# A decoder layer in fp32 on one core: the banded branch of half 0 by seven products in place of eight, with its sums of outputs made beside the last gate tiles

## The chip, the cores and the metric

The kernel runs on one core of a Trainium2 chip. The metric is the device time of one execution in microseconds (us); "before" is the median of three runs. The core has five engines that run at the same time, each its own instruction stream: TensorE (PE, with PEld for its weight loads), VectorE (DVE), ScalarE (ACT), GpSimd (POOL) and SyncE (SP). SP issues nearly all transfers between device memory and SBUF, on one queue, in order. TensorE writes only to PSUM, which has eight banks here; VectorE and ScalarE empty them.

## The reference, cut to what matters

A hybrid decoder layer: 2048 tokens with 16 meta tokens ahead of them, width 1024. One input projection yields queries, keys and values of two attentions, and gates. The stick-breaking attention has 8 heads of 64, the banded one ("sliding window", 128 wide) 16. What comes after them is what the change touches:

```python
y_sb = (o_sb * jax.nn.silu(sb_z)) @ w_branch_sb[l]     # 512 -> 1024
y_sw = (o_sw * jax.nn.silu(sw_z)) @ w_branch_swa[l]    # 1024 -> 1024, the "banded branch"
merged = jax.nn.sigmoid(g_sb) * y_sb + jax.nn.sigmoid(g_sw) * y_sw
h = h + merged @ w_out[l]
return rms_norm(h, final_norm_gain)[:, BLOCK:]
```

## The kernel before, in words

Every tile has 128 partitions. The tokens are taken in four groups of 512 columns, in reverse order, in two halves: half 0 is groups 2 and 3, half 1 is groups 0 and 1. Each fp32 operand x is split into a high part h (a rounded copy, fp32r) and a low part l = x - h, and each product is three matmuls that add up in one bank: h.h, h.l and l.h. A tile of 128 output columns with 1024 inputs is thus 8 x 3 = 24 matmuls of 512 columns per group.

`tile_kernel` computes projections and attentions of half 0, then of half 1, and last `finish` (line 235) for both halves. The gates (silu of sb_z and sw_z, sigmoid of g_sb and g_sw) are tiles of the input projection; `gate` (line 612) takes such a product from a bank with the tag "g" (two banks), applies ScalarE's sigmoid (line 615) and, for silu, a product on VectorE (line 617), and stores it to device memory (`zs`, `zw`, `gs`, `gw`). Attention outputs lie there too (`ow` banded, `od` stick-breaking).

The last five gate tiles of half 1 (the last of g_sw and four of sb_z) come after all attention, in the loop at line 1457. After each of the first four, the kernel makes ready four of the 16 tiles of gated banded outputs of half 0: `gated` (line 206) loads output and gate, multiplies (217), copies the high part (ScalarE, 219) and subtracts for the low part (VectorE, 220); they stay in SBUF as `ringl`. Line 1469 splits the first weight tile of w_sw (`weights`, line 178, with `split`, line 112). Then the buffers of x and of temporary tiles are given back (`fst.close()`), and `finish` takes that place for its own.

In `finish`, for each half: (1) the banded branch, for each of eight tiles d of 128 columns and each of the two groups 24 matmuls (`project`, lines 258 to 260, reading `ringl`), then a product with the gate `gw` (286) into `part`; the weights are split on GpSimd (lines 117 and 123) and in half 0 also stored in split form, which half 1 loads again; (2) between, the outputs of the other branch (`od`) made ready in the same way, into `ringr` (277); (3) the other branch, 12 matmuls per tile and group, reading `ringr`, product with `gs`, sum with `part`, split into `merged` (296 to 300); (4) the product with w_out (336 to 338), residual, norm, store. Weights of w_out are split by `out_weights` (265), the second half of them after the first output tile (349). While half 0's outputs are made, half 1's banded outputs are made ready in place (`gated_in_place`).

The order on TensorE is that of the program text. The order on VectorE, ScalarE, GpSimd and SP is chosen by a scheduler that models their times, except where the code says `manual_schedule`; each engine then works its list off in order, and an instruction waits for semaphores of the others.

Of the kernel before, what the change touches and what calls it, by code (L numbers as in the profile page):

```python
# [43 lines left out]
def f32(ap):  # L44
    return ap.bitcast(F32)
# [3 lines left out]
def tile_kernel(ctx, tc, x, xt, meta, metat, gain, w_in, w_sb, w_sw, w_out, sinks, fgain,  # L49
# [6 lines left out]
    V, A, G, T = nc.vector, nc.scalar, nc.gpsimd, nc.tensor  # L56

    def DMA(dst, src):
        nc.sync.dma_start(*(t.bitcast(F32) if t.dtype == F32R else t for t in (dst, src)))
# [34 lines left out]
    def dram(name, shape, dt=F32):  # L94
        return dp.tile(shape, dt, tag=name, name=name)
# [79 lines left out]
        DMA(raw, w[c0 // P])  # L175
        return raw

    def weights(c0, w=w_in, raw=None, split=split):
# [11 lines left out]
        split(wh, wl, raw)  # L190
        kept[key] = [dram(f"{t}_{w.name}_{c0}", [P, n, P], F32R) for t in "hl"]
# [9 lines left out]

    def rings():
        lp = cst.enter_context(tc.tile_pool(name="cl", bufs=1, side="left"))
        return lambda dt=F32R: lp.tile([P, GT], dt, tag="L", name="ringl", bufs=32)

    def gated(src, zz, k, g, ring, stg):

# [24 lines left out]
        V.tensor_tensor(l, t, f32(h), op=ALU.subtract)  # L232
        return h, l

    def finish(ringl, osw, first):
        cp = cst.enter_context(tc.tile_pool(name="wb", bufs=1, side="right"))
        banks = iter(range(1 << 30))

        def bank():
            return ps("gzt"[next(banks) % 3])  # L240

        def ringr(dt=F32R):
            return cp.tile([P, GT], dt, tag="R", name="ringr", bufs=40)

        def small(tag, bufs):
            return cp.tile([P, GT], F32, tag=tag, name=tag, bufs=bufs)
# [15 lines left out]
        for half, groups in enumerate(halves):  # L262
            part, merged, wo = {}, {}, {}

            def out_weights(k, ch):
                raw = small("a", AB)
                DMA(raw, w_out[0, k * P:(k + 1) * P, ch * GT:(ch + 1) * GT])
                h, l = wo[k, ch] = ringr(), ringr()
                A.copy(h, raw)
                V.tensor_tensor(l, raw, f32(h), op=ALU.subtract)  # L270

            osw2 = {}
            ws_of = {}
            order = [(d, g) for ds in ([0, 1, 2], *([d] for d in range(3, 8))) for g in groups for d in ds]
            for d, g in order:
                if d == 3 and g == groups[0]:
                    osb = {(k, g): gated(od, zs, k, g, ringr, lambda: small("a", AB)) for g in groups for k in range(4)}
                if d not in ws_of:
                    ws_of[d] = first if half == d == 0 else weights(d * P, w_sw)
# [4 lines left out]
                DMA(gt, gw[d][g])  # L284
# [4 lines left out]
            for d in range(8):  # L289
                ws = weights(d * P, w_sb)  # L290
                for g in groups:
                    acc = bank()
                    project(acc, ws, [osb[k, g] for k in range(4)])
                    gt = small("gt", 3)
                    DMA(gt, gs[d][g])
                    V.tensor_tensor(gt, acc, gt, op=ALU.mult)
                    V.tensor_tensor(gt, gt, part[d, g], op=ALU.add)  # L297
                    mh, ml = merged[d, g] = ringl(), ringl()
                    A.copy(mh, gt)  # L299
                    V.tensor_tensor(ml, gt, f32(mh), op=ALU.subtract)  # L300
                if d < 6:
                    out_weights(d + 2, 0)
            for g in groups:
                for t0 in range(0, 4, 2):
                    res, ssq, scaled_by = {}, {}, {}
# [12 lines left out]
                    for ch in range(2):  # L318
                        cs = slice(ch * GT, (ch + 1) * GT)
                        for t in (t0, t0 + 1):  # L320
                            row = g * GT + t * P
                            if ch == 0:
                                res[t] = cp.tile([P, D], F32, tag="xr", name="res", bufs=3)
                                DMA(res[t], x[row:row + P, :])
                            ts = slice(t * P, (t + 1) * P)
                            last = end and t == 3
                            if ch == 0:
                                ssq[t] = cp.tile([P, 2], F32, tag="ssq", name="ssq2", bufs=4)
                            sum_of = ssq[t][:, ch:ch + 1]
# [19 lines left out]
                            if (g, t, ch) == (groups[0], 0, 0):  # L349
                                for k in range(KT):  # L350
                                    out_weights(k, 1)
# [44 lines left out]
    def sums():  # L396
        return tp.tile([P, 2, 4], F32, tag="ssq", name="ssq", bufs=3)
# [953 lines left out]
    for half, groups in enumerate(halves):  # L1351
# [100 lines left out]
            mid.close()  # L1452
        else:
            ringl = rings()
            osw = {}
            todo = [(k, g) for g in halves[0] for k in range(8)]
# [10 lines left out]
            for k, g in todo:  # L1467
                osw[k, g] = gated(ow, zw, k, g, ringl, tmp)
    first = weights(0, w_sw)
    fst.close()  # L1470
    finish(ringl, osw, first)
    cst.close()

_OUT = (2048, 1024)
# [45 lines left out]
```

## Time and profile before

| | us |
|---|---|
| median of 3 runs (2090.64 to 2091.54) | 2091.31 |
| the profiled execution's own time | 2093.26 |
| its span, first to last instruction | 2091.4 |
| TensorE busy in the span | 2076.3 |
| VectorE busy | 1463.0 |
| ScalarE busy | 1091.4 |
| GpSimd busy | 345.7 |

The profile comes from one execution, whose time is 1.95 us above the median of the others. A matmul's record is longer than the step to the next one, because matmuls overlap; so a busy TensorE says that there was no gap, and the step from start to start gives the price. In rows of a stretch the engines are PE, PEld, DVE, ACT and POOL, each with its busy time and number of instructions; behind them stand the granted TensorE clock (1.00 is full), the busy share of the 16 DMA engines, and GB/s. In rows of single instructions stand start, duration, engine, line, operation, what it writes and reads, its shapes, and in brackets how long the engine was idle before and whom it waited for.

### The profile page before, as it was taken

The page shows a single profiled execution, that of the slowest core. Times are in us where ns is not written, and L with a number is a line of the kernel's source. Part 1 is how long each engine was busy: PE and PEld are TensorE (multiplying, and loading weights), DVE is VectorE, ACT ScalarE, POOL GpSimd, SP SyncE. Part 2 cuts the span into 40 slices and gives each one's busy share as a digit, 9 for nine tenths or more (in the row PEclk, how much of TensorE's full clock was granted, in tenths as well). Part 3 has the DMA queues.
Part 4 walks back from the last instruction along what each step waited for, and adds up shares of the span by engine and source line. Part 5 has one row for each costly group of instructions (what it writes and reads, how often), then busy time and mean ns, then how long its engine had stood idle before and what let it go on. Part 6 is the DMA issues. An engine that isn't in the chain of part 4 may idle for free. (4 is left out here: it accounts for less than half of the span.)

```text
span 2091.4 us, 30949 instructions
## 1 busy us (share of the span) xinstructions
PE 2076.3 (99%) x10579; PEld 1744.8 (83%) x10579; DVE 1463.0 (70%) x2383; ACT 1091.4 (52%) x2657; POOL 345.7 (17%) x682
## 2 busy tenths in 40 slices
PE   9999999999999999999999999999999999999998
PEld 7888888888888888888888888888888888788887
DVE  7897986877687754887728788777774547464543
ACT  6677774577665335777735555655653212321121
POOL 1233444331000000233310000000000343000000
PEclk9999999999999999999999999999999999999999
DMA  9855555866377574435455344343424987568532
GB/s 338 307 195 201 188 175 179 252 199 185 91 278 298 209 247 163 159 126 177 150 171 161 120 130 129 114 129 98 121 83 165 350 318 223 182 229 305 154 100 91
DMA packets 170093, 391.46 MB, mean 187 GB/s; under 512 B 23728, under 2 KB 28208, under 8 KB 169936
## 3 DMA queue, kind: packets, MB, share of 16 engines
q1 hardware_dynamic: 169648, 389.23, 55.8%
q8 instruction: 83, 1.36, 0.3%
q14 instruction: 74, 0.61, 0.1%
q10 hardware_dynamic: 288, 0.27, 0.0%
HBM read 241.68 MB, written 145.18 MB: 185 GB/s over the span
## 5 line engine op out<-in xcount | busy, mean ns | idle before, releaser
L464 PE MATMUL ps_g<-xh,wh 128*128 128x512 f32 x1264 | 517.0, 409 | 1.1 <-DVE tmp L680 0.6
L464 PE MATMUL ps_g<-xl,wh 128*128 128x512 f32 x1264 | 495.6, 392 | 0.7 <-DVE xl L1199 0.6
L464 PE MATMUL ps_g<-xh,wl 128*128 128x512 f32 x1264 | 495.7, 392 | 0.0
L928 DVE TENSOR_TENSOR_SCAN row<-row 128x512 f32<-128x512 f32 (+4 forms) x256 | 290.1, 1134 | 116.2 <-POOL row L923 60.1
L464 PEld LDWEIGHTS ps_g<-xh,wl 128*128 128x128 f32 x1264 | 237.8, 188 | 52.7
L464 PEld LDWEIGHTS ps_g<-xh,wh 128*128 128x128 f32 x1264 | 238.5, 189 | 39.9 <-ACT xh L1198 1.4
L464 PEld LDWEIGHTS ps_g<-xl,wh 128*128 128x128 f32 x1264 | 239.2, 189 | 38.0 <-DVE xl L1199 1.8
L921 ACT ACTIVATE row<-ps_z 128x512 f32<-128x512 f32 (+4 forms) x352 | 175.1, 509 | 159.3 <-PE ps_z L918 155.0
L126 ACT ACTIVATE wth<-ps_t 128x512 fp32r<-128x512 f32 (+1 forms) x320 | 171.6, 536 | 61.4 <-PE ps_t L943 59.6
L127 DVE SCALAR_TENSOR_TENSOR wtl<-ps_t,wth 128x512 fp32r<-128x512 f32 (+1 forms) x320 | 188.7, 590 | 21.3 <-ACT wth L126 20.7
L918 PE MATMUL ps_z<-kt,q 128*128 128x512 f32 (+4 forms) x704 | 183.7, 349 | 2.0 <-ACT row L921 1.9
L943 PE MATMUL ps_t<-ident,row 128*128 128x128 f32 x1088 | 171.4, 273 | 1.0 <-DVE wtl L127 0.9
L943 PEld LDWEIGHTS ps_t<-ident,row 128*128 128x128 f32 x1088 | 134.5, 140 | 33.1 <-DVE wtl L127 1.8
L918 PEld LDWEIGHTS ps_z<-kt,q 128*128 128x128 f32 x704 | 124.4, 188 | 27.4 <-ACT row L921 5.1
L975 PE MATMUL ps_o<-wth,vc 128*128 128x512 f32 (+1 forms) x320 | 131.2, 410 | 0.0
L975 PE MATMUL ps_o<-wtl,vc 128*128 128x512 f32 (+1 forms) x320 | 116.4, 364 | 0.0
L767 ACT ACTIVATE sc<-sc,nm 128x129 f32<-128x129 f32 x256 | 100.0, 393 | 30.5 <-DVE nm L765 29.5
L934 POOL COPY mr<-row 128x16 f32<-128x16 f32 x128 | 28.4, 224 | 444.2 <-DVE row L928 401.8
L615 ACT ACTIVATE tmp<-ps_g 128x512 f32<-128x512 f32 x80 | 48.0, 600 | 80.5 <-PE ps_g L464 74.3
L299 ACT CAST ringl<-gt 128x512 fp32r<-128x512 f32 x32 | 19.9, 621 | 127.1 <-DVE gt L297 93.3
L117 POOL TENSOR_SCALAR wh<-raw 128x1024 fp32r<-128x1024 f32 (+1 forms) x45 | 49.8, 1108 | 212.7 <-PE ps_g L464 90.3
L123 POOL TENSOR_TENSOR wl<-raw,wh 128x256 fp32r<-128x256 f32 x88 | 83.2, 975 | 2.0
(442 smaller groups left out, 4202.3 us busy)
## 6 DMA issues: line engine op xcount, KB each, us to landing
wh<-h_in_w_in SPq DMA_DIRECT2D x66, 512.0 KB, 3.9
wl<-l_in_w_in SPq DMA_DIRECT2D x66, 512.0 KB, 5.1
h_in_w_in<-wh SPq DMA_DIRECT2D x50, 512.0 KB, 3.3
l_in_w_in<-wl SPq DMA_DIRECT2D x50, 512.0 KB, 4.1
raw<-in_w_in SPq DMA_DIRECT2D x49, 512.0 KB, 5.3
q<-qd SPq DMA_DIRECT2D x128, 128.0 KB, 3.2
vc<-vd SPq DMA_DIRECT2D x48, 256.0 KB, 3.2
kd<-tmp SPq DMA_DIRECT2D x32, 256.0 KB, 3.4
```

What stands on the lines that cost most here:

```text
L117: G.tensor_scalar(h, src, 1.0, 1.0, op0=ALU.mult, op1=ALU.mult)
L123: G.tensor_tensor(l[:, c], src[:, c], f32(h[:, c]), op=ALU.subtract)
L126: A.activation(h, acc, AF.Copy, scale=scale)
L127: V.scalar_tensor_tensor(l, acc, scale, f32(h), op0=ALU.mult, op1=ALU.subtract)
L464: T.matmul(acc, lhsT=a[:, k, :], rhs=b[:, k, :], start=k == i == 0, stop=k == KT - 1 and i == 2)
L615: A.activation(e, acc, AF.Sigmoid)
L767: A.activation(sc[:, hh, :], sc[:, hh, :], AF.Exp, bias=nm[:, hh:hh + 1], accum_out=den[:, hh:hh + 1])
L918: T.matmul(z[:, :m], lhsT=qt[:, j * P:(j + 1) * P], rhs=kt[h][:, k0 + c:k0 + c + m], start=t == 0, stop=t == 1)
L921: A.activation(r[:, c:c + m], z[:, :m], AF.Sigmoid, scale=-1.0)
L928: V.tensor_tensor_scan(r[:, :w], r[:, :w], r[:, :w], last[j] if n else 1.0, op0=ALU.mult, op1=ALU.min)
L943: T.transpose(tr[:, j * P:(j + 1) * P], rows_of[h, g, n - (j > i), j][:, k0:k0 + P], ident)
L975: T.matmul(o[:, :n], lhsT=v, rhs=r, start=first and r is wh, stop=last)
```

## The change

Half 0's banded branch is computed in pairs of output tiles and the two groups at once, with a scheme of seven half-size products for a 2 x 2 block product (outputs B11, B21, B12, B22: two halves of the 1024 inputs by two groups; weights: the same two halves by two tiles) in place of eight. It needs sums of output blocks (t1 to t4) and sums of weight blocks.

- `outputs_blocks` takes the place of `gated` beside the last gate tiles: for each k of four it loads and multiplies four outputs and gates, makes four sums, and splits seven blocks (b11, b21, t1, b22, t2, t3, t4). t4 of every k and t3 of the last k are stored to device memory and loaded again by `finish`.
- `weight_blocks` loads w_sw tiles in pairs and yields 14 split half-tiles for four tiles; for the first two blocks the split is on GpSimd (`fill_early`), for the others on ScalarE and VectorE (`fill`), and the sums of weights are on VectorE. Two blocks are made ahead of `finish`, and one more is asked for at each step.
- `branch_by_pairs` runs the products. Partial sums stay in banks with the tag "o" over several products and are copied away by ScalarE in between (`keep`).
- The other branch's outputs of half 0 are made ready at set points (`hook`).
- Half 1 keeps the old products, but loads w_sw anew and splits it, since half 0 no longer stores it in split form.
- The second half of w_out is loaded and split before the output stage, not after its first tile. Buffers: `ringl` 43 in place of 32, `ringr` 29 in place of 40.

The core of the diff:

```diff
+    def outputs_blocks(blk, away, k, ga, gb, ring, stg, zed):
...
+        b11, b21, b12, b22 = (product(kk, g) for g in (ga, gb) for kk in (k, k + HK))
+        t3 = stg()
+        put("b11", b11)
+        put("b21", b21)
+        V.tensor_tensor(t3, b22, b12, op=ALU.subtract)
+        V.tensor_tensor(b12, b12, b11, op=ALU.subtract)
+        put("t1", b12)
+        put("b22", b22)
+        V.tensor_tensor(b22, b22, b12, op=ALU.subtract)
+        put("t2", b22)
+        V.tensor_tensor(b21, b21, b22, op=ALU.subtract)
+        put("t3", t3, away if k == HK - 1 else None)
+        put("t4", b21, away)
+
+    def weight_blocks(spare_raw, sums):
...
+        for c in (0, 4):
+            one, two = (quarters(load(d * P, w_sw)) for d in (c, c + 2))
+            put = fill if c else fill_early
+            for i in range(2):
+                w = new_tile()
+                yield put(w, 0, one[i]), put(w, 1, two[i])
+            low = second(c + 1)
+            r, q = sums(), sums()
+            V.tensor_tensor(r, low[0], low[1], op=ALU.add)
+            V.tensor_tensor(q, r, one[0], op=ALU.subtract)
+            w = new_tile()
+            yield fill(w, 0, r), fill(w, 1, q)
...
+    def branch_by_pairs(groups, blk, ahead, blocks, part, bank, new, gate_of, hook):
...
+        def keep(d, g, acc):
+            t = part[d, g] = new(d, g)
+            A.copy(t, acc)
+
+        def gated_sum(d, g, acc):
+            t = part[d, g]
+            V.tensor_tensor(t, acc, t, op=ALU.add)
+            V.tensor_tensor(t, t, gate_of(d, g), op=ALU.mult)
...
+            za = ps("o")
+            product(za, w[0], "b11", True)
+            keep(a, ga, za)
...
+            zb = ps("o")
+            product(zb, w[1], "b11", True)
+            keep(b, ga, zb)
+            w = fetch()
+            for d, wi in zip((a, b), w):
+                acc = bank()
+                product(acc, wi, "b21", True, True)
+                gated_sum(d, ga, acc)
+            hook(c, 0)
+            w = fetch()
+            x = bank()
+            product(x, w[0], "t1", True)
+            keep(a + 1, gb, x)
+            product(za, w[1], "t2")
+            keep(a, gb, za)
+            w = fetch()
+            product(x, w[0], "b22", stop=True)
+            gated_sum(a, gb, x)
+            product(za, w[1], "t3")
+            gated_sum(a + 1, gb, za)
+            hook(c, 1)
...
+                for key in (("t3", HK - 1), *(("t4", k) for k in range(HK))):
+                    blk[key] = ringr(), ringr()
+                    for t, d in zip(blk[key], away[key]):
+                        DMA(t, d)
...
-                for k, g in todo[:4]:
-                    osw[k, g] = gated(ow, zw, k, g, ringl, tmp)
-                del todo[:4]
...
+                for k in todo[:1]:
+                    made.extend(ringl() for _ in range(min(12, 43 - len(made))))
+                    ring = slots((made + [wm[0], wm[1], columns(vm[:, 0:2])])[12 * k:])
+                    outputs_blocks(blk, away, k, *halves[0], ring, tmp, ring_x)
+                del todo[:1]
...
+    blocks = weight_blocks(lambda: raws[0](), lambda: raws[1]())
+    ahead = [next(blocks), next(blocks)]
     fst.close()
-    finish(ringl, osw, first)
+    finish(ringl, blk, away, blocks, ahead, raws)
```

More of the change, by code (lines that the diff above doesn't have):

```diff
@@ L176, in load, with weights @@
         return raw
-    def weights(c0, w=w_in, raw=None, split=split):
+    def weights(c0, w=w_in, raw=None, split=split, keep=True):
         if c0 in ready:
@@ L190, in weights @@
         split(wh, wl, raw)
+        if not keep:
+            return wh, wl
         kept[key] = [dram(f"{t}_{w.name}_{c0}", [P, n, P], F32R) for t in "hl"]
@@ L233, in gated_in_place, with part_split, slots, columns @@
         return h, l
-    def finish(ringl, osw, first):
+    def part_split(h, l, t):
+        A.copy(h, t)
+        V.tensor_tensor(l, t, f32(h), op=ALU.subtract)
+    def slots(tiles):
+        it = iter(tiles)
+        return lambda: next(it)
+    def columns(t):
+        return t.rearrange("p a b c -> p (a b c)")
+    def outputs_blocks(blk, away, k, ga, gb, ring, stg, zed):
+        def product(kk, g):
+            a, z = stg(), zed()
+            DMA(a, ow[kk][g])
+            DMA(z, zw[kk][g])
+            V.tensor_tensor(a, a, z, op=ALU.mult)
+            return a
+        def put(name, t, out=None):
+            if out is None:
+                h, l = blk[name, k] = ring(), ring()
+                part_split(h, l, t)
+                return
+            h = stg().bitcast(F32R)
+            l = t.bitcast(F32R)
+            A.copy(h, t)
+            V.tensor_tensor(l, t, f32(h), op=ALU.subtract)
+            away[name, k] = [dram(f"{name}{i}{k}", [P, GT], F32R) for i in "hl"]
+            for u, d in zip((h, l), away[name, k]):
+                DMA(d, u)
+        b11, b21, b12, b22 = (product(kk, g) for g in (ga, gb) for kk in (k, k + HK))
[11 more added lines that the diff above has]
+        put("t4", b21, away)
@@ L236, in finish @@
+    def finish(ringl, blk, away, blocks, ahead, raws):
         cp = cst.enter_context(tc.tile_pool(name="wb", bufs=1, side="right"))
         banks = iter(range(1 << 30))
+        loaded = [None]
         def bank():
@@ L242, in ringr @@
         def ringr(dt=F32R):
-            return cp.tile([P, GT], dt, tag="R", name="ringr", bufs=40)
+            return cp.tile([P, GT], dt, tag="R", name="ringr", bufs=29)
         def small(tag, bufs):
@@ L266, in out_weights @@
                 raw = small("a", AB)
-                DMA(raw, w_out[0, k * P:(k + 1) * P, ch * GT:(ch + 1) * GT])
-                h, l = wo[k, ch] = ringr(), ringr()
+                loaded[0] = DMA(raw, w_out[0, k * P:(k + 1) * P, ch * GT:(ch + 1) * GT]).ins
+                ring = ringl if k < 3 and ch == 1 - half else ringr
+                h, l = wo[k, ch] = ring(), ring()
                 A.copy(h, raw)
@@ L283, in finish @@
                 gt = small("gt", 3)
-                DMA(gt, gw[d][g])
+                with tc.issue_after(loaded[0]):
+                    DMA(gt, gw[d][g])
                 part[d, g] = ringr(F32)
@@ L288, in finish @@
                 out_weights(d, 0)
[L289 to L302, printed above, removed]
+            ws_of = {}
+            for d, g in [(d, g) for ds in ([0, 1], *([d] for d in range(2, 8))) for g in groups for d in ds]:
+                if d not in ws_of:
+                    ws_of[d] = weights(d * P, w_sb)
+                acc = bank()
+                project(acc, ws_of[d], [osb[k, g] for k in range(4)])
+                for f in rest:
+                    f()
+                rest = []
+                gt = small("gt", 3)
+                DMA(gt, gs[d][g])
+                V.tensor_tensor(gt, acc, gt, op=ALU.mult)
+                V.tensor_tensor(gt, gt, part[d, g], op=ALU.add)
+                mh, ml = merged[d, g] = ringl(), ringl()
+                A.copy(mh, gt)
+                V.tensor_tensor(ml, gt, f32(mh), op=ALU.subtract)
+                if g == groups[1]:
+                    for k, ch in ((d + 2, 0),) if d < 6 else ((0, 1),) if d == 6 else ((1, 1), (2, 1)):
+                        out_weights(k, ch)
+            for k in range(3, KT):
+                out_weights(k, 1)
             for g in groups:
@@ L1454, in tile_kernel @@
             ringl = rings()
-            osw = {}
-            todo = [(k, g) for g in halves[0] for k in range(8)]
+            blk, away, made = {}, {}, []
+            todo = list(range(HK))
             for mk in gts[rest:]:
@@ L1463, in tile_kernel @@
                     drain(tiles_by_tile([mk], groups))
[L1464 to L1469 removed]
+                for k in todo[:1]:
[3 more added lines that the diff above has]
+                del todo[:1]
+            assert not todo
+    raws = []
+    blocks = weight_blocks(lambda: raws[0](), lambda: raws[1]())
+    ahead = [next(blocks), next(blocks)]
     fst.close()
[L1471 removed]
+    finish(ringl, blk, away, blocks, ahead, raws)
     cst.close()
```

111 lines of the change are left out of this document (103 added, 8 removed).

## Prediction

> **What bounds the kernel now.** I read first the busy times of the page, then the stretches around the part that changes, then single instructions of TensorE, VectorE, ScalarE and the DMA queue there.
>
> ```profile
> PE 2076.3 (99%) x10579; PEld 1744.8 (83%) x10579; DVE 1463.0 (70%) x2383; ACT 1091.4 (52%) x2657; POOL 345.7 (17%) x682
> ```
>
> ```profile
> 1600.00:1647.00 47.00, 47.00 (x209) 38.92 (x208) 25.06 (x34) 12.31 (x22) 9.97 (x10) 1.00 0.86 301
> 1647.00:1690.00 43.00, 43.00 (x192) 35.59 (x191) 20.64 (x25) 6.08 (x9) 19.50 (x20) 1.00 1.00 380
> 1690.00:1734.00 44.00, 44.00 (x196) 36.44 (x195) 15.94 (x20) 4.78 (x8) 13.88 (x16) 1.00 0.74 251
> ```
>
> TensorE (second figure) has no gap in the last gate tiles (1600 to 1647) nor in the banded branch of half 0 (1647 to 1734). So a microsecond is won only by fewer matmuls, and lost wherever TensorE now has to wait. VectorE, busy half of 1600 to 1647, does its waiting free of charge.
>
> **1. What goes.** Line 258 shows the branch reading `ringl` and then the other branch reading `ringr`:
>
> ```profile
> L258 PE MATMUL ps_g<-ringl,wh x96: 389/389/389, 1647.6 to 1953.1; 128*128 128x512 f32 x96
> ...
> L258 PE MATMUL ps_z<-ringr,wh x48: 389/389/389, 1734.6 to 1996.6; 128*128 128x512 f32 x48
> ```
>
> From 1647.6 to 1734.6 are 87.0 us for 384 matmuls (8 tiles x 2 groups x 24): 0.2266 us each (the 389 ns overlap), 5.44 per group of a tile. Seven products of 12 per pair of tiles make 336: 48 fewer, as the instruction counts of the two programs also say (10579 and 10531). **-10.9 us.** The one gap in the output stage, in the view of line 336, goes too, since the second half of w_out is now loaded earlier: **-0.5**.
>
> ```profile
> its engine sat idle before it (us, times) until:
>   ACT ringr L269: 0.5, 1
> ```
>
> **2. The sums beside the last gate tiles.** For each quarter VectorE now has 15 operations ahead of the gate's own (4 gate products, 4 sums, 7 low parts); before it was 8 in the same time. In the order of instructions, ScalarE's sigmoids of a gate tile stand behind all seven high-part copies, and the products that empty the gate's banks behind all 15. Gates have two banks ("g"), so the next gate tile cannot start until then. How this runs now:
>
> ```profile
> 1604.28 0.60 ACT L615 ACTIVATE tmp<-ps_g 128x512 f32<-128x512 f32 x1 [4.84 <-PE ps_g L464]
> 1609.79 0.60 ACT L615 ACTIVATE tmp<-ps_g 128x512 f32<-128x512 f32 x1 [4.90 <-PE ps_g L464]
> 1611.09 0.62 ACT L219 CAST ringl<-tmp 128x512 fp32r<-128x512 f32 x1 [0.71 <-DVE tmp L217]
> ```
>
> ```profile
> 1610.37 0.69 DVE L217 TENSOR_TENSOR tmp<-tmp 128x512 f32<-128x512 f32 x1 [17.96 <-DMA tmp<-ow]
> ...
> 1616.48 0.69 DVE L617 TENSOR_TENSOR tmp<-ps_g,tmp 128x512 f32<-128x512 f32 x1
> ```
>
> ```profile
> L220 DVE TENSOR_TENSOR ringl<-tmp,ringl 128x512 fp32r<-128x512 f32 x16 | 14.8, 928 | 3.7 <-ACT ringl L219 3.4
> L217 DVE TENSOR_TENSOR tmp<-tmp 128x512 f32<-128x512 f32 x16 | 12.1, 755 | 26.6 <-DMA tmp<-ow 18.0 <-DMA tmp<-zw 8.2
> ```
>
> ```profile
> tmp<-ow SPq DMA_DIRECT2D x16, 256.0 KB, 5.2
> ```
>
> The first loads land at 1610.4 as now; nine operations to 1616.48 give 0.68 each. 15 and the bank's own end at 1610.4 + 16 x 0.68 = 1621.3. TensorE wants that bank one group after 1609.8, at 1615.2: it waits **6.1**. The tile runs 10.9, to 1632.2. VectorE, after the second bank (1622.0), needs 16 x 0.75 (the mean of L217, with GpSimd's weight splits beside it): 1634.0, a wait of **1.8**. The third quarter's loads reuse buffers that the second has just left, so they are issued at about 1634; they land after 5.2 (median now) or, unloaded, about 2.5. I take 4: 1638 + 12.0 = 1650.0, wanted at 1644.9, **5.1**. Sum **+13.0**. Ends: 2.9 (rival B) and 24.9 (rival D). The last quarter delays no bank, because the branch starts on others.
>
> **3. The wait for the third weight block.** Let T be the end of the last gate matmul. The fifth product (t1) needs a sum from tile 1 of w_sw. Its load goes into memory that gate buffers held, and on SP it stands behind fg and ten reloads (t3, t4), which all wait for the last gate's store. That order exists now:
>
> ```profile
> 1653.37 0.32 SPq L59 DMA_DIRECT2D zs<-tmp  x1
> ...
> 1655.57 0.33 SPq L59 DMA_DIRECT2D fg<-in_fgain  x1
> ```
>
> Gate emptied T+2.5 (the last 15 operations end 1.1 after T, and two follow); the store takes 2.2; fg, ten of 0.26 MB and the tile are 3.67 MB, at 380 GB/s (row 1647 to 1690) 9.7; 1.5 of latency (2.2 less 0.7 of streaming). The tile lands at R = T+15.9. Sum 0.69, copy 0.62: T+17.2. Four products of 2.72 are done at T+10.9. Wait 6.3, and 1.0 more for the low part, which stands behind two operations: **+7.3**. Ends 0 (all lands earlier, rival C) and 10.
>
> The Trainium skill, "DMA: Bandwidth & Descriptors", section "Where 436 GB/s comes from", puts HBM to SBUF at about 358 GB/s for a core. This trace does not agree (380 over 43 us in the row above); by the page the stretch would be 10.2, and R later by an estimated 0.5.
>
> **4. The wait for the kept partial sum.** The product "b22" accumulates into the bank whose first value ScalarE must copy away (`keep`). In ScalarE's order that copy stands behind seven weight copies and two copies of the other branch (`hook`), the second of which waits for the 22nd VectorE operation counted from R. 22 x 0.61 to 0.69 (start to start, or whole) is 13.4 to 15.2, two copies 1.2: R+14.6 to R+16.4. TensorE has done t1 and t2 at R + 2.3 + 5.4 = R+7.7. Wait 6.9 to 8.7, taken **+8.0**. The ends are below that if the order is less strict than it reads (0), above if od's loads are later (12).
>
> **5. Small waits.** The bank of the pair left over is closed and at once reused (a product of VectorE, 0.69, and its signal), some t4 low parts arrive late: **+2.5**, between 0 and 6. For 14 products (38.1) VectorE has 14 low parts, 8 weight sums, 14 operations on banks and 12 of the other branch, 48 x 0.65 = 31: covered by the products, apart from the order of steps 3 and 4; without that cover they would be waits. On the DMA queue 16 stores of split w_sw tiles and 8 of 16 half-megabyte loads in half 1 go, ten stores and ten reloads of 0.26 MB come; only the reloads stand ahead of something urgent (step 3). Half 1 now loads raw w_sw and splits it (4 low parts on GpSimd per 10.9 us) in place of two loads: TensorE covers it, 0, at worst 4.
>
> **6. The clock.** At the start the trace shows what waiting costs afterwards:
>
> ```profile
> 12.00:16.00 4.00, 4.00 (x16) 3.19 (x15) 2.69 (x5) 3.15 (x7) 0.00 (x0) 0.77 1.09 329
> ```
>
> ```profile
> 10.14 0.59 PE L464 MATMUL ps_g<-xl,wh 128*128 128x512 f32 x1 [0.62 <-DVE xl L1199]
> 10.53 0.63 PE L464 MATMUL ps_g<-xh,wh 128*128 128x512 f32 x1
> ...
> 13.52 0.54 PE L464 MATMUL ps_g<-xh,wl 128*128 128x512 f32 x1
> ...
> 14.12 0.39 PE L464 MATMUL ps_g<-xh,wh 128*128 128x512 f32 x1
> 14.35 0.39 PE L464 MATMUL ps_g<-xh,wl 128*128 128x512 f32 x1
> ```
>
> Seven steps at 0.43 in place of 0.23: 1.4 us lost. I charge that once for each of the four gaps over 3 us (6.1, 5.1, 6.3, 8.0): **+5.6**; ends 0 and 8. The Trainium skill, "TensorE: Matmul & The Clock Gate", section "Why this matters for your kernels", says that one idle window (about 3 us) halves the clock. The slow steps agree, though here gaps of 0.6 us sufficed; by its window of 3.4 us the estimate is 1.7 a gap, 6.8 in all.
>
> **The sum.** -10.9 - 0.5 + 13.0 + 7.3 + 8.0 + 2.5 + 5.6 = +25.0. The profiled execution took 2093.26 (span 2091.4), 1.95 more than the median of the runs, 2091.31; so 2118.3 profiled, and **2116** beside that median.
>
> **Rivals.**
>
> A, the forecast: all waits as above, 2116. For it: both orders are written, engines work them off in order, and the rows give the paces. Against: the landing times are those of another order. Chance 0.66.
>
> B, light waits: VectorE keeps 0.61 and loads land 2.2 after issue. Gates: first load at 1607.0, bank at 1616.8, waits 1.6, 0 and 1.3; third block 5.2 + 0.8; kept sum 6.9; small 1.0; two clock charges 2.8. 19.6 - 11.4 = +8.2: 2099.5. The 5.2 of the loads speaks against it. Chance 0.14.
>
> C, the other side: the reloads do not hold up the weight tile, because the 16 engines work on all of them at once; it lands 2.2 after fg. Place: the third block. R = T + 1.5 + 2.2 + 2.2 = T+5.9: no wait for t1; the kept sum comes at R+14.6 = T+20.5 against T+16.3, 4.2. With B's gates 2.9, small 1.0 and one clock charge 1.4 that is 9.5, less 11.4: -1.9, 2089.4. It decides the sign as soon as all waits together stay below 11.4. The full DMA share (1.00) now at that place speaks against it. Chance 0.07, of which 0.05 is faster by over 0.2% (4.2 us, about what a measurement can tell) if the kept sum is in time as well.
>
> D, crowded VectorE: 0.93 per operation through the gates (L220's mean, GpSimd beside it). Bank at 1625.3, waits 10.1, 5.9, 8.9: 24.9 in place of 13.0, 2128. Chance 0.13.
>
> That the change does not do what it says is excluded by the counts.
>
> **How the numbers follow.** Slower by over 0.2%: A, B and D, 0.93, less 0.01 for B's lower end: 0.92. Faster: 0.05 of C. Within 0.2%: the other 0.02 of C and B's 0.01, 0.03. The range reaches from 2097 (below B) to 2131 (above D), leaving out C and the tails of B and D.
>
> **What would show it.** Waits of TensorE for VectorE ahead of the second and fourth of the last four gate tiles, 5 to 6 us each, and a small one ahead of the third: step 2. A wait of about 6 after the fourth product of the branch, released by ScalarE: step 3. One of about 8 ahead of the seventh: step 4. Granted clock below 1 behind them: step 6. If the branch and the gates show no waits, -11.4 alone would stand, 2080, and the reading of the orders is wrong. If half 1 waits for its weights, I missed a cost.

## The result, and the profile after

| | us |
|---|---|
| changed kernel, median of 4 runs (2118.96 to 2125.64) | 2122.36 |
| kernel before, the runs beside them, median of 4 (2090.64 to 2092.11) | 2091.43 |
| ratio, with its 95% interval | 1.0148 (1.0127 to 1.0169) |
| profiled execution of the changed kernel, its span | 2125.11, 2123.4 |

The change costs 1.5%. It was forecast at 2116, between 2097 and 2131.

Line numbers from here on are those of the changed kernel: 687 is the projection's matmul, 838 and 840 the gate's sigmoid and product, 239 and 265 low parts of blocks, 348 to 350 the products of the new branch (`product`), 354 `keep`, 358 and 404 the operations of VectorE that empty a bank of that branch, 291 and 292 the high and low parts of its weights, 318 to 336 sums of weights, 221 the high copy of an output for the other branch, 442 to 444 the products of the other branch, 519 to 523 the steps that make `merged`, 115 and 455 the high copies of w_sw for half 1 and the low parts of w_out, 562 to 564 the outputs. In kernels with edits some move by a few lines. From the page, the line of busy times:

```profile
PE 2076.5 (98%) x10531; PEld 1741.3 (82%) x10531; DVE 1507.6 (71%) x2463; ACT 1125.1 (53%) x2713; POOL 347.2 (16%) x686
```

TensorE issues the 48 matmuls fewer, but its busy time has not fallen (2076.3 before), because some of its steps are now longer. Where the 32.0 us of span (2123.4 against 2091.4) came from is read from three stretches, cut at the first matmul of each stage: the last gate tiles, the banded branch with the other branch, the outputs of half 0. Start and end, length, then PE, PEld, DVE, ACT and POOL, the granted clock, DMA share, GB/s. Before:

```profile
1593.20:1647.60 54.40, 54.40 (x241) 45.04 (x240) 25.64 (x35) 14.74 (x28) 9.97 (x10) 1.00 0.85 294
1647.60:1778.16 130.56, 130.56 (x577) 108.11 (x576) 75.06 (x98) 21.28 (x35) 49.25 (x54) 1.00 0.83 288
1778.16:1866.70 88.54, 87.98 (x386) 71.83 (x384) 43.74 (x99) 24.16 (x62) 0.00 (x0) 1.00 0.53 176
```

After:

```profile
1591.12:1663.17 72.05, 59.95 (x242) 48.48 (x240) 45.59 (x67) 22.35 (x42) 10.27 (x12) 0.91 0.66 223
1663.17:1803.99 140.82, 124.99 (x530) 101.35 (x528) 94.54 (x142) 41.38 (x69) 25.69 (x28) 0.95 0.72 241
1803.99:1899.12 95.13, 89.62 (x386) 73.20 (x385) 48.23 (x104) 25.80 (x64) 7.58 (x8) 0.96 0.50 167
```

The same 240 gate matmuls take 17.65 longer. The branches, with 528 matmuls in place of 576, take 10.26 longer, where 10.9 less was to be had. The outputs take 6.59 longer. Together 34.5; the profiled execution was 2.1 ahead when the first stretch began (1591.12 against 1593.20), and won 0.4 more behind the third (224.28 to the end of the span against 224.70). Half 1's banded and other branch took 130.55 against 130.56 before.

TensorE's waits after the change, as sum, number and longest:

```profile
PE ps_g L687 <- DVE tmp L840: 12.1, 2, 6.2
PE ps_t L348 <- ACT wh L291: 7.2, 1, 7.2
PE ps_t L348 <- ACT ringr L354: 5.8, 1, 5.8
PE ps_g L562 <- ACT ringl L522: 5.0, 1, 5.0
PE ps_o L348 <- DVE ringr L358: 1.9, 1, 1.9
...
PE ps_o L348 <- DVE ringr L404: 0.8, 1, 0.8
...
PE ps_g L564 <- DVE ringl L523: 0.5, 1, 0.5
```

The first three were forecast by place and releaser. The fourth was not: it lies inside the first output product, after 21 of its 24 matmuls, where the last tile of `merged` is read for the first time (the texts of the runs call this place "ahead of the first output product"). Behind each long wait the steps are slow. Single matmuls around the second wait in the gates (start, duration, and in brackets the idle time):

```profile
1643.07 0.39 PE L687 MATMUL ps_g<-xh,wl 128*128 128x512 f32 x1
1649.67 0.79 PE L687 MATMUL ps_g<-xh,wh 128*128 128x512 f32 x1 [6.22 <-DVE tmp L840]
1650.27 0.63 PE L687 MATMUL ps_g<-xl,wh 128*128 128x512 f32 x1
...
1654.96 0.41 PE L687 MATMUL ps_g<-xh,wh 128*128 128x512 f32 x1
1655.21 0.39 PE L687 MATMUL ps_g<-xl,wh 128*128 128x512 f32 x1
```

From 1649.67 to 1655.21 are 13 steps, 12 of them slow, in 5.54 us, where 13 x 0.2266 = 2.95 would do: 2.6 lost behind one wait.

### The profile page after: what moved, and what is told of

Same layout as the page of the kernel before. It is cut to its first block, busy times and chain, and to the rows that moved or that the text cites. A ratio compares the mean times of both kernels' runs of the same rounds, so it can differ in the third digit from the quotient of the medians.

```text
span 2123.4 us, 31022 instructions
## 1 busy us (share of the span) xinstructions
PE 2076.5 (98%) x10531; PEld 1741.3 (82%) x10531; DVE 1507.6 (71%) x2463; ACT 1125.1 (53%) x2713; POOL 347.2 (16%) x686
## 5 line engine op out<-in xcount | busy, mean ns | idle before, releaser
L687 PE MATMUL ps_g<-xh,wh 128*128 128x512 f32 x1264 | 518.6, 410 | 13.4 <-DVE tmp L840 12.1
L127 DVE SCALAR_TENSOR_TENSOR wtl<-ps_t,wth 128x512 fp32r<-128x512 f32 (+1 forms) x320 | 188.7, 590 | 21.3 <-ACT wth L126 20.7
L574 ACT ACTIVATE sq<-res 128x512 bf16<-128x512 f32 (+1 forms) x33 | 20.4, 618 | 125.3 <-DVE res L566 125.3
L1149 DVE TENSOR_TENSOR_SCAN row<-row,mask 128x512 f32<-128x512 f32 (+2 forms) x64 | 70.0, 1100 | 17.4 <-ACT row L1144 16.9
```

The costliest lines, as they stand in the source:

```text
L127: V.scalar_tensor_tensor(l, acc, scale, f32(h), op0=ALU.mult, op1=ALU.subtract)
L687: T.matmul(acc, lhsT=a[:, k, :], rhs=b[:, k, :], start=k == i == 0, stop=k == KT - 1 and i == 2)
L1149: V.tensor_tensor_scan(r[:, :w], r[:, :w], mask[:, :w], 1.0, op0=ALU.mult, op1=ALU.max)
```

## The experiments

The theory: each wait has a cause of its own in the order of VectorE's, ScalarE's and SP's work. The rivals differ by run. Each profile is of one execution, so its waits are read as to place and rough size; times are medians.

### Gates: more banks, and an earlier start

In banks4 the calls for a bank in the last five tiles go to two tags:

```diff
-yield from lagged(col_tile(w, g, use, ...))
+yield from lagged(col_tile(w, g, use, ..., bank=next(last_banks)))   # last_banks = iter('gz' * 8)
```

> The last five gate tiles take banks with the tags "g" and "z" in turn, four banks in place of two; nothing else differs from the changed kernel. Theory (VectorE's 15 operations a quarter start late and are too long; the banks only show it): the gate tiles run without a wait (12.1 us of waits and some 5 of slow clock go), but the last gate's store, and with it the third weight block, comes at most 3 us sooner, so the wait for ScalarE ahead of the fifth product grows from 7.2 to 20 us (17 to 24); the wait of 5.8 ahead of the seventh stays. Time 2114 to 2121, against 2122.4. Rival (two banks are the cause): the gate waits go, the later ones stay as they are, 2105.

Measured: 2118.85 (2117.83 to 2121.12), ratio 1.0135 (1.012 to 1.015). The gates run in 54.40 without a wait, and the waits of banks4 in the branch are:

```profile
PE ps_t L348 <- ACT wh L291: 16.3, 1, 16.3
PE ps_t L348 <- ACT ringr L354: 4.9, 1, 4.9
```

Of the 17.65 us gained in the gates 9.1 came back in one wait (16.3 lies just below the 17 to 24 expected), and 12.8 in the whole stretch of the branches (1645.89 to 1799.50, 153.61 against 140.82). Most of the debt had only moved on, and the two-bank rival (2105) falls.

early4 adds the earlier start:

```diff
 for mk in gts[rest:]:
+    for k in todo[:1]: ... outputs_blocks(blk, away, k, ...)
     drain(tiles_by_tile([mk], groups))
-    for k in todo[:1]: ... outputs_blocks(blk, away, k, ...)
```

> Each quarter of the sums is issued ahead of its gate tile, one tile earlier than in the changed kernel, and the gate tiles take four banks as in banks4. Theory (late start): no gate wait, the wait ahead of the fifth product stays at 7 to 9 us, the one ahead of the seventh at 6 to 8: 17 us less, 2106 (2102 to 2110). Rival (VectorE is too slow for 17 operations a tile, wherever they start): waits in the gates or ahead of the first products of the branch remain, 5 us or more together, and the time is above 2112.

Measured: 2114.59 (2109.96 to 2119.93), ratio 1.0122 (1.0104 to 1.0139); the profiled execution is the fastest of the four, 2109.96. The median misses the 2102 to 2110 of the theory and lies above the rival's 2112. Two waits of early4, and VectorE beside GpSimd's weight splits:

```profile
PE ps_t L348 <- ACT wh L291: 7.8, 1, 7.8
...
PE ps_g L687 <- DVE tmp L840: 3.2, 1, 3.2
```

```profile
1625.27 2.37 DVE L239 TENSOR_TENSOR ringl<-tmp,ringl 128x512 fp32r<-128x512 f32 x2
```

The fifth product waits as long as with the late start, as the theory says. But 3.2 are left in the gates: two operations take 2.37 here, where two take 1.29 without GpSimd, and VectorE falls behind a tile of 10.9 us. Both sides hold a part. Gates and fifth product together waited 19.3 in the changed kernel, 16.3 in banks4 and 11.0 here, where the fifth product's 7.2 have another cause. So of 12.1 us the earlier start with its banks leaves 3.8: by these profiles the late start was most of it, and the crowded VectorE the rest.

### The third weight block

reload makes the third block, and with it the load of its w_sw tile, before the ten reloads:

```diff
+ahead.append(next(blocks))            # in finish, ahead of the reloads
 for key in (("t3", HK - 1), *(("t4", k) for k in range(HK))):
...
+if len(ahead) < 3:                     # in fetch
     ahead.append(next(blocks, None))
```

> The third weight block, with the load of its w_sw tile, is issued ahead of the ten reloads of t3 and t4; the gates are as in the changed kernel. Theory (the reloads ahead of it on SP's queue make the tile late, and what follows is a chain of VectorE and ScalarE work that starts when it lands): the wait ahead of the fifth product falls from 7.2 to under 1.5, but the one ahead of the seventh grows from 5.8 to 9 to 12, since TensorE now comes there sooner; net 2 to 5 us less, 2118. Rival 1 (two independent waits): the seventh stays at 5.8, 2113. Rival 2 (all transfers share the engines, their order does not matter): the fifth still waits 5 us or more.

Measured: 2117.36 (2113.57 to 2120.56), ratio 1.0126 (1.0111 to 1.0141). The wait ahead of the fifth product is gone, and that ahead of the seventh is twice what it was:

```profile
PE ps_t L348 <- ACT ringr L354: 11.5, 1, 11.5
```

So the order on SP is what made the tile late, and the two waits are one chain seen twice: 7.2 + 5.8 = 13.0 became 11.5. Rivals 1 and 2 fall. In the changed kernel the chain reads (SP's issues, VectorE, ScalarE):

```profile
1672.96 0.44 SPq L59 DMA_DIRECT2D ringr<-t4l  x1
1673.46 0.40 SPq L59 DMA_DIRECT2D res<-in_w_sw  x1
...
1680.03 0.69 DVE L318 TENSOR_TENSOR a<-res 128x512 f32<-128x512 f32 x1 [5.02 <-DMA res<-in_w_sw]
...
1693.48 0.62 ACT L291 CAST wh<-a 128x512 fp32r<-128x512 f32 x1 [2.92 <-DVE a L334]
1694.08 0.62 ACT L221 CAST ringr<-a 128x512 fp32r<-128x512 f32 x1
1694.60 0.58 ACT L354 COPY ringr<-ps_t 128x512 f32<-128x512 f32 x1
```

The tile's load is issued behind the last reload and lands at 1680.0; the copy out of the bank (354) stands behind a weight copy and a copy for the other branch, and ends at 1695.2.

### The copy out of the bank

lateod moves all work for the other branch's outputs to the second four tiles:

```diff
-if c == 0: ...       # two k of the first group at each call
-elif n == 0: ...     # four k of the second group
+if c == 4:
+    for k in (2 * n, 2 * n + 1):
+        other_branch(k, groups[0], ringr)
+        other_branch(k, groups[1], ringl)
```

> The other branch's outputs of half 0 are made ready during the second four tiles of the banded branch alone, not during the first; the gates and the reloads are as in the changed kernel. Theory (the copy out of the bank stands behind the work on the other branch's outputs): the wait ahead of the seventh product falls from 5.8 to under 1, and with it 2 us of slow clock; up to 2 us come back late in the branch: 2115 (2113 to 2118). Rival (the copy waits for the weight copies of the fourth and fifth block): a wait of 4 us or more stays, 2120 or more.

Measured: 2120.29 (2118.14 to 2124.45), ratio 1.0143 (1.0128 to 1.0158). This is above the 2113 to 2118 of the theory and just above the rival's 2120, and its 2.1 us below the changed kernel lie within the spread of four runs, so only the profile decides. There the wait ahead of the seventh product is gone (the row of ScalarE's 354 on "ps_t" is no more there): the other branch's work does hold the copy up. But the scheduler also put the copy in another place. On ScalarE six weight copies stand ahead of it between the tile's landing and the copy, where eight stood in the changed kernel. So the rival is not excluded as a part of the cause: the run does not tell whether the other branch's copies alone made the wait, or together with the two weight copies. And the same kind of copy now comes late for the last pair of tiles:

```profile
PE ps_z L348 <- ACT ringl L354: 3.2, 1, 3.2
```

It is the same kind of wait in another place, with its own slow steps behind it. These explain a part of the 5 us above the middle of the expectation; the rest stays open.

### The clock

fill puts unneeded matmuls into the two waits of the branch, the first into the bank that the fifth product starts anew, the others into a free one:

```diff
+fill_idle(x, 29)          # ahead of the fifth product
 product(x, w[0], "t1", True)
...
+fill_idle(bank(), 23)     # ahead of the seventh
 product(x, w[0], "b22", stop=True)
```

> The changed kernel with matmuls that compute nothing needed (29 ahead of the fifth product, 23 ahead of the seventh) put into the two waits of the banded branch; all else as in the changed kernel. Theory (TensorE's own idling sets the slow steps that follow): the waits shrink from 7.2 to about 0.7 and from 5.8 to about 0.7, the products behind them start at the same moments, but at 0.227 us a step from the first on, granted clock 1.00 there: about 2 us less for each, 2118. Rival (the slow steps come from what the engines or the memory do at that moment): steps of 0.43 us stay behind both, no gain.

Measured: 2121.6 (2120.02 to 2124.16), ratio 1.0149 (1.0136 to 1.0163). The matmuls behind the two waits in fill:

```profile
1679.99 0.50 PE L348 MATMUL ps_t<-ringl,wh 128*128 128x512 f32 x1 [0.82 <-ACT wh L291]
...
1682.34 0.39 PE L348 MATMUL ps_t<-ringl,wh 128*128 128x512 f32 x1
1682.56 0.40 PE L349 MATMUL ps_t<-ringl,wh 128*128 128x512 f32 x1
...
1693.83 0.50 PE L348 MATMUL ps_t<-ringl,wh 128*128 128x512 f32 x1 [2.02 <-ACT ringr L354]
...
1695.41 0.63 PE L350 MATMUL ps_t<-ringl,wl 128*128 128x512 f32 x1
1695.83 0.63 PE L348 MATMUL ps_t<-ringl,wh 128*128 128x512 f32 x1
```

Behind the wait that was filled but for 0.82 the steps are 0.23 (apart from a wait of 0.58 for a low part); behind the other, where 2.02 were left, they are slow from 1694.63 to 1698.0. The other engines and the transfers did the same work as before, so it is TensorE's idling that sets the slow steps. But no time was won, where 2118 was expected: from the fifth to the seventh product 13.84 us pass with the fill (1679.99 to 1693.83) and 13.81 without (1681.43 to 1695.24), because the seventh waits for ScalarE, whose chain hangs on the tile's landing. A slow stretch that ends in another wait costs nothing.

### The outputs

gsfirst orders half 1's loads behind half 0's last gate load; wout_late puts the second half of w_out back behind the first output tile:

```diff
-DMA(gt, gs[d][g])                            # gsfirst
+last_gate = DMA(gt, gs[d][g]).ins
...
+loaded[0] = last_gate
```

```diff
-for k, ch in ((d + 2, 0),) if d < 6 else ((0, 1),) if d == 6 else ((1, 1), (2, 1)):    # wout_late
+for k, ch in ((d + 2, 0),) if d < 6 else ():
...
+if (g, t, ch) == (groups[0], 0, 0):
+    for k in range(KT):
+        out_weights(k, 1)
```

> Half 1's first loads of raw w_sw and gates wait for the issue of half 0's last gate load, in place of the last w_out load; all else as in the changed kernel. Theory (half 1's raw tiles are issued ahead of the last gate loads on SP and make VectorE and GpSimd busy just then): the wait ahead of the first output product, 3.4 to 5.0 in the four profiles with the late start, falls below 1, and 2 us of slow clock go: 2116. Rival (the second half of w_out, now split ahead of the output stage, does it): the wait stays at 3 us or more, and the run wout_late takes it away.

> The second half of w_out of half 0 is loaded and split after the first output tile again, as before the change; all else as in the changed kernel. Rival of gsfirst (16 more operations on ScalarE and VectorE ahead of the last outputs): the wait ahead of the first output product falls below 1, 2116. Theory of gsfirst: it stays at 3 us or more. If both runs take it away, the two work together.

Measured: gsfirst 2116.56 (2114.59 to 2120.11), ratio 1.0126 (1.0112 to 1.014), with 1.4 us of the wait left and 91.11 for the stretch; wout_late 2115.18 (2113.3 to 2116.09), ratio 1.0117 (1.0101 to 1.0132), with none:

```profile
1801.76:1888.80 87.04, 87.04 (x385) 72.10 (x384) 45.31 (x99) 26.27 (x65) 9.29 (x12) 1.00 0.59 207
```

87.04 is 384 x 0.2266: this stretch is 8.1 below the changed kernel's 95.13. In the changed kernel, SP's issues, VectorE and ScalarE:

```profile
1792.07 0.42 SPq L59 DMA_DIRECT2D raw<-in_w_sw  x1
1792.59 0.45 SPq L59 DMA_DIRECT2D gt<-gs  x1
...
1798.62 0.69 DVE L519 TENSOR_TENSOR gt<-ps_z,gt 128x512 f32<-128x512 f32 x1 [3.65 <-DMA gt<-gs]
...
1810.91 1.21 DVE L523 TENSOR_TENSOR ringl<-gt,ringl 128x512 fp32r<-128x512 f32 x1
1812.04 1.20 DVE L520 TENSOR_TENSOR gt<-gt,ringl 128x512 f32<-128x512 f32 x1
...
1813.28 0.62 ACT L522 CAST ringl<-gt 128x512 fp32r<-128x512 f32 x1 [4.08 <-DVE gt L520]
```

The gate tile issued at 1792.59, right behind half 1's first raw tile, lands 6.0 later; VectorE idles 3.65 for it, and then has the last tiles of `merged` and the w_out splits to catch up at up to 1.2 us an operation, GpSimd beside it. In gsfirst ScalarE does this ahead of the wait that is left:

```profile
1807.72 1.04 ACT L115 CAST wh<-raw 128x1024 fp32r<-128x1024 f32 x1 [1.82 <-DMA raw<-in_w_sw]
1808.67 1.14 ACT L522 CAST ringl<-gt 128x512 fp32r<-128x512 f32 x2
```

The last two copies for `merged` stand behind a copy of half 1's raw weights, which waits for their landing. So half 1's raw weights hold the first 3.6 us, as gsfirst shows, and by these rows the 1.4 that are left too. wout_late does not test the w_out splits alone: half 1's loads wait for the last load of w_out, so that edit moves them as well (the first is issued at 1813.41 there, after the outputs have begun). Whether the earlier splits of w_out hold a part of the wait stays open.

### Edits together

all4 is early4, reload, lateod and gsfirst in one kernel.

> Four edits together: sums a tile earlier with four banks, third weight block ahead of the reloads, the other branch's outputs in the second four tiles, half 1's loads behind the last gate load. Theory (each wait has a cause of its own, and removing one does not merely move it to the next): of the waits only some 3 us in the gates, 2 ahead of the fifth product and 3 later in the branch stay, with 3 us of slow clock: 2091 (2086 to 2097), level with the kernel before. Rival (VectorE and ScalarE have too much to do between the gates' end and the seventh product, so waits only move): above 2103.

Measured: 2094.8 (2093.22 to 2097.14), ratio 1.002 (1.0012 to 1.0029). The time is inside the expected range, but 0.2% above the kernel before, not level with it. Alone the four edits won 7.8, 5.0, 2.1 and 5.8, which is 20.7 us; together 27.6. Each of the four is a difference of medians of four runs, which lie up to 10 us apart, so the comparison is rough; it agrees with the traces, where what one edit wins is partly taken by the next wait. Left over:

```profile
PE ps_z L348 <- ACT ringl L354: 4.4, 1, 4.4
PE ps_g L688 <- DVE tmp L841: 4.2, 1, 4.2
```

spread6 takes six banks (`'gzt'`), and hands three of the other branch's eight outputs to a new call of `hook` behind the last b22 product.

> all4 with two edits more: the last gate tiles take six banks (g, z and t in turn), and three of the other branch's eight outputs are made ready only after the second four tiles' last b22 product. Theory (a wait that sits on a chain fixed by another engine moves on when it is taken away): the gates run without a wait (4.2 us and 2 us of slow clock go), but VectorE's last gate products end at most 2 us sooner, so a wait of about 4 us comes up ahead of the fifth product, where all4 had 0.3; the wait of 4.4 late in the branch goes with 2.6 us of slow clock: 2088 (2086 to 2091). Rival (the fifth product's weights come in time anyway): 2083.

Measured: 2095.27 (2093.01 to 2096.78), ratio 1.0021 (1.0011 to 1.003). Both waits are gone, and there is

```profile
PE ps_t L348 <- ACT wh L291: 6.2, 1, 6.2
PE ps_g L563 <- ACT ringl L522: 2.5, 1, 2.5
```

instead: the wait moved on, as the theory says, and is larger than its 4; and the one at the outputs came back, where TensorE arrives 5 us earlier (1776.53 against 1781.47). The waits taken away (8.6) and those that came (8.7) are equal, and the time is that of all4, not the 2088 expected.

best6 takes the third block off that chain:

```diff
 if c == 0 and i == 1:
+    low = quarters(load(P, w_sw))      # into the second raw tile's buffer
...
+    two = second(c + 2)                # that tile again, later
```

> spread6 with one edit more: the raw tile from which the third weight block is summed is loaded before the branch, into the buffer of the second raw tile, which is loaded again later; so its load stands behind no store and no reload. Theory (the third block was late because its tile's memory came free only with the last gate store): the wait ahead of the fifth product goes, no wait above 2.5 us is left in the branch, and the time is 2083 (2081 to 2086), below the kernel before by more than 0.2%. Rival (then VectorE's own sums are late): a wait of 3 us or more at the fifth or seventh product, 2087 or more.

Measured: 2094.99 (2092.3 to 2096.88), ratio 1.0018 (1.0009 to 1.0027). The wait ahead of the fifth product fell to 1.2, but the raw tiles of the fifth block now landed late behind the same reloads:

```profile
PE ps_g L354 <- ACT wh L291: 3.0, 1, 3.0
PE ps_g L569 <- ACT ringl L528: 2.5, 1, 2.5
```

It did not reach 2083. The last kernel removes these two: reloads behind the loads of the fifth block, w_out as in wout_late.

> best6 with two edits more: the ten reloads of t3 and t4 are issued behind the loads of the two raw tiles for the fifth block (in best6 that block was late: waits of 3.0 and 1.2 us and 1.5 us of slow clock), and the second half of w_out is made ready after the first output tile again, as in wout_late, in place of the order of half 1's loads (in best6 a wait of 2.5 us ahead of the first output product and 2 us of slow clock). Theory (every wait left has a cause in the order of transfers and sums): no wait above 1.5 us from the gates to the outputs, 10 us below best6: 2085 (2082 to 2088), faster than the kernel before by 0.1 to 0.4%. Rival (VectorE and ScalarE have too much work for half 0's branch, so that a new wait comes up): a wait of 2 us or more and 2089 or above.

Measured: 2085.62 (2084.55 to 2087.1, 10 runs) against 2090.74 of the kernel before in the same rounds, ratio 0.9976 (0.9967 to 0.9986). The three stretches of best7, and two of its waits:

```profile
1591.93:1646.33 54.40, 54.40 (x241) 45.06 (x240) 41.62 (x59) 18.89 (x37) 13.07 (x12) 1.00 0.79 271
1646.33:1773.47 127.14, 121.86 (x530) 98.50 (x528) 102.31 (x154) 43.64 (x75) 21.53 (x24) 1.00 0.77 265
1773.47:1860.51 87.04, 87.04 (x386) 72.10 (x384) 45.31 (x99) 26.28 (x65) 9.28 (x12) 1.00 0.60 206
```

```profile
PE ps_o L354 <- DVE ringl L364: 1.8, 2, 1.2
...
PE ps_t L354 <- ACT wh L291: 1.2, 1, 1.2
```

The seven products with the sums beside them beat both kernels, the kernel before by 0.24%, once their transfers and copies stand in the right order. The clock is 1.00 in all three stretches, and no wait is above 1.2. Of the 10.9 us for the matmuls, 3.4 are won in the branches (127.14 against 130.56); the waits left there, 5.3 in all, and the longer steps behind them (121.86 busy, where 528 x 0.2266 = 119.6 would do) hold the rest. The outputs give 1.5 more (87.04 against 88.54), which do not come from the seven products.

## Why the forecast held, step by step

| step | forecast | measured in the profiled execution |
|---|---|---|
| 1, fewer matmuls | -10.9 | -10.9 (counts, same step) |
| 1, gap in the output stage | -0.5 | +6.6: a new wait and slow steps |
| 2, gates | +13.0 | +12.1 |
| 3, third block | +7.3 | +7.2 |
| 4, kept sum | +8.0 | +5.8 |
| 5, small waits | +2.5 | +2.7 |
| 6, slow steps in gates and branch | +5.6 | about +11 (17.65 - 12.1 and 10.26 + 10.9 - 15.7) |
| start and end of the execution | 0 | -2.5 |

**Step 2** gave 6.1, 1.8 and 5.1; the run shows 5.88, none and 6.22. Its mechanism is as written: in the changed kernel the product that empties the bank stands behind the last low part.

```profile
1617.58 0.68 DVE L265 TENSOR_TENSOR tmp<-tmp 128x512 fp32r<-128x512 f32 x1
1618.18 1.28 DVE L840 TENSOR_TENSOR tmp<-ps_g,tmp 128x512 f32<-128x512 f32 x2
```

The second wait vanished since VectorE started that quarter at 1619.4, not 1622.0, and kept about 0.65 an operation. In the third quarter two errors met: its loads landed 2.3 sooner than forecast (VectorE starts at 1635.74, not 1638), and its 16 operations took 13.9 in place of 12.0, for GpSimd's splits ran beside them (rival D's pace, but in one quarter of three). That the sum came out at 12.1 is in part luck.

**Steps 3 and 4** had the right queues (reload and lateod). I put the tile's landing at T+15.9; T is 1663.2 and VectorE starts on it at 1680.03, T+16.9. Rival C, that the reloads do not hold it up, is excluded by reload. Two errors offset each other there: the last gate's store was done at T+3.8, not T+4.7, and from fg's issue to the tile's landing 13.0 passed, not 11.2. Step 4's copy ended at R+15.2, inside the 14.6 to 16.4 (eight weight copies stood ahead of it, not seven), but TensorE reached the wait at R+9.4, not R+7.7, held up by the slow steps behind the fifth product. So the wait was 5.8 in place of 8.0, and the 1.4 that step 6 charged for the gap of step 3 was already inside step 4's 8.0. Treating 7.3 and 8.0 as two prices was right for the sum, since each was counted from the same landing, but they are not two savings.

**Step 1's second part** is the step that failed. It read the earlier second half of w_out as a gap saved, and priced half 1's raw weights at nothing because TensorE has time in half 1. Half 1 did not wait for them (130.55 against 130.56). But both are started in half 0's other branch, where VectorE has three operations per 2.7 us product, and the raw weights delay the last tiles of `merged` there: gsfirst, which moves only them, takes 3.6 of the 5.0 us. The share of the w_out splits is not shown. The gap of 0.5 did not hang on their order alone, for wout_late has them in the old place and no gap; what removed it stays open. The working did not ask what is queued behind the work it moved; the answer, the last `merged` tiles, stands in the order of SP, VectorE and ScalarE.

**Step 6** was mis-sized: the right mechanism, 1.4 us a gap taken from the kernel's start (seven steps), where 8 to 12 slow steps followed the four waits, 2.0 to 2.6 us (as worked out above for one of them). Nor do the gaps of 0.6 us at the start say what a single gap does later: single gaps of 0.8 to 1.6 us were followed by no slow step in these profiles. The Trainium skill, "TensorE: Matmul & The Clock Gate", section "Why this matters for your kernels", puts the limit at gaps of about 3 us. The runs here put it lower: 2.02 sufficed in fill and 2.5 in spread6 and best6, though 2.41 in banks4 did not.

The misses of steps 1 and 6 (+7.1 and +5) were partly made up by step 4 (-2.2), step 2 (-0.9) and the start (-2.5). That is why 2116 lies only 6 us off. Step 4's share belongs to step 6, as said; the other 3.4 us are luck, and what made the start 2.1 us earlier was not tried.

## What to carry to other kernels

Price work that is moved into another stage by what stands behind it in that stage's queues, on every engine and on the DMA queue, whatever TensorE's cover there. When a wait hangs on a chain that another engine or a landing tile fixes, filling or removing an earlier wait only moves it: find the event the chain starts from (here one load behind ten that were less urgent) and move that. A saving of few matmuls in a kernel without gaps is real only when all new waits are taken out together: here it took all the edits of best7 to win 3.4 of the 10.9 us in the branches.

## What was not expected of the hardware

- The slow steps: 0.43 in place of 0.227 us, 6 to 14 of them, behind every wait of 2.46 us or more in these twelve profiles from the gates to the outputs. Around 2 us it goes either way: 2.02 in fill was followed by seven, 2.41 in banks4 and 1.93 in the changed kernel by none. Two short waits close together can count as one (1.42 and 0.45 in gsfirst were followed by seven); single ones of 0.8 to 1.6 were followed by none. Their number does not grow with the wait (12 behind 5.88 and 8 behind 7.22 in the changed kernel, 14 behind 4.9 and 13 behind 16.3 in banks4).
- Executions of some kernels with such waits scatter more: 2118.96 to 2125.64 in four runs of the changed kernel and 2109.96 to 2119.93 in four of early4, against 2084.55 to 2087.1 in ten of best7. It is no rule: four runs of banks4, with the longest wait of all, lie within 3.3 us, and 15 of the kernel before within 5.0. What varies between them was not tried and stays open.
- Two-input operations on VectorE took 1.0 to 1.2 us in place of 0.61 to 0.69 where GpSimd split weights at the same time, and 1.29 for two where it did not. The Trainium skill, "SBUF — State Buffer", section "SBUF: two separate sides", says that GpSimd and a VectorE operation with two SBUF inputs lock each other out of a shared port pair; these rows agree, and the operation at 1801.18 in the changed kernel (line 519, one input in PSUM) took 0.69 between two of 1.22 and 1.10, GpSimd busy beside all three.
